# A log-sum-exp kernel: SyncE issues the first load ahead of the opening barrier

## The chip, the cores and the metric

One core of one Trainium2 chip. The metric is the device time of one execution in microseconds (us); the median of several executions is given, with its range. All executions of this study were in the fast state, with a granted clock of 1.00. A ratio is the mean time of one kernel's fast runs over the mean of the other kernel's fast runs in the same rounds, so it is not quite the ratio of the medians quoted beside it.

## The reference

```python
# x: float32 [32, 512, 1024]
max_x = np.max(x, axis=-1, keepdims=True)
return (max_x.squeeze(-1) + np.log(np.sum(np.exp(x - max_x), axis=-1))).astype(np.float32)
```

There are 16384 rows of 1024 numbers, 67.1 MB to read and 64 KB to write. Each of the 128 partitions holds 128 rows, `NC` in the code.

## The kernel before

The kernel reads the input once, through a ring of 48 rows per partition in SBUF. SyncE issues all loads; ScalarE takes the exponential in place; VectorE adds up most rows, and ScalarE itself some of them. The sums are taken without subtracting the maximum. A check at the end looks for sums that are out of range, and a slow path, not taken here, would repair them.

```python
    RING = 48
    loads = [
        "R8 R8", "R8 R8", "R8 R8", "R7 R6 A A", "R6 R5 A A A", "R5 R4 A", "R5 R4", "R5 T3",
        "R3 A A A", "R3 A", "R2 T2", "R3", "R1 A", "T2", "T1", "A", "A",
    ]                       # one string is one load; R: exp, then VectorE adds; A: ScalarE adds
# ... cut: the other tiles
    ring = big.tile([P, RING, d], fp32, name="ring")
    nc.scalar.preload_act_table_set("natural_log_exp_and_others")
    nc.vector.memset(ones, 1.0)
    nc.vector.memset(far, 100 * HIGH)

    def load(p0, c0, size):
        return nc.sync.dma_start(out=ring[:, p0 : p0 + size, :], in_=x_rows[:, c0 : c0 + size, :])
# ... cut
    for ops in loads:
        size = sum(s for _, s in ops)
        if p + size > RING:
            p = 0
        dma = load(p, c, size).ins
        for how, s in ops:
            v = ring[:, p : p + s, :]
            # ... cut: exp in place; reduce_sum of v on VectorE, or the accumulator of ScalarE
            c += s
            p += s
        tc.add_to_no_dep_group("loads", dma)
# ... cut
    nc.scalar.activation(out=res[:, EARLY:NC], in_=sumexp[:, EARLY:NC], func=AF.Ln)
    nc.sync.dma_start(out=out_view, in_=res)
# ... cut: the check of the sums, and the slow path
```

The opening of the program is not in this source. It begins with a barrier of all five engines: each engine executes a drain that reports to GpSimd, GpSimd sets four constants in memory, waits for the four reports, and releases all. Only then do the engines branch to the block that holds the code above. In the source above, the first three loads fill the ring (16 + 16 + 16 rows) and wait for no data and no slot; from the fourth on, a load waits until a slot is free.

## Time and profile before

| | before |
|---|---|
| time, median of the 3 runs known ahead of the prediction | 165.37 us (165.01 to 165.41) |
| span of the profiled execution (its own time: 164.92 us) | 163.1 us |
| first load issued / first data packet / sixteenth engine's first packet | 0.73 / 1.73 / 3.23 us |
| one 64 KB packet on one of the 16 DMA engines, steady | 2.42 us |
| last load has landed / tail after it | 159.01 / 4.1 us |

The span starts with the first instruction that the profile shows, which is SyncE's drain. The packets' times and the landing are from the trace's records of single DMA packets and of semaphore increments. A packet is a 64 KB piece, one partition's 16 rows in a large load. The records don't name the engine; the first 16 packets are taken to be on 16 engines, because all of them start before any of them ends.

From the page of the kernel before: the span; the busy share of the DMA engines in 40 slices of 4.08 us, in tenths; the rate in each slice; and the share that each engine has in the chain that ended last.

```profile
span 163.1 us, 198 instructions
...
DMA  6979989998998999899999999999999999999970
GB/s 257 514 321 450 514 370 402 514 418 354 514 418 354 514 438 407 377 482 482 450 394 422 436 420 402 402 450 434 434 418 442 422 440 400 426 423 421 409 314 18
...
DMA 64%; DVE 22%; ACT 12%; issue 1%; SPq 0%; PE 0%; DVEq 0%
```

The DMA engines are busy in every slice but the last, which is the tail after the loads. The first slice, with 257 GB/s, is short because the stream has not begun until 1.73 us, and the last two because it ends in them. The others scatter (321 to 514 GB/s) because whole packets are counted where they start. The chain names VectorE for 22%, because it follows loads back to the reductions that freed their slots; it doesn't say that the stream had run empty there.

From the table of waits of SyncE (what it waited for: us in total, how often, the longest) and of ScalarE:

```profile
SPq L72 <- DVE sumexp L99: 88.3, 7, 24.3
SPq L72 <- DMA ring<-in_x_dram: 41.1, 4, 20.9
...
SPq L197 <- PEq L197: 0.7, 1, 0.7
```

```profile
ACT ring L92 <- DMA ring<-in_x_dram: 42.9, 9, 21.0
```

SyncE waits 88 us for free slots, but all of this happens while earlier loads are in flight. The last line of SyncE's is the one at issue here: 0.7 us at the opening barrier, before any load. ScalarE waits 42.9 us for data.

From the instructions of the barrier, all under one source line (engine, operation, count; duration in ns, lowest/median/highest; first and last start in us; a "q" marks the engine's sequencer):

```profile
L197 POOLq EVENT_SEMAPHORE  x2: 17/17/17, 0.5 to 0.6; - x2
L197 SPq DRAIN  x1: 7/7/7, 0.0 to 0.0; - x1
...
L197 POOLq DRAIN  x1: 181/181/181, 0.3 to 0.3; - x1
...
L197 SPq EVENT_SEMAPHORE  x1: 17/17/17, 0.7 to 0.7; - x1
```

SyncE is at its drain at 0.0 us and passes the barrier at 0.65 us (0.7 as printed). GpSimd's own drain, which ends behind its four constants at 0.49 us, is what the others wait for.

From the timeline (start, duration, engine, line, operation):

```profile
0.24 0.10 POOL L197 MEMSET const-float32-0.0<- 128x1 f32 x1 [0.24 <-issue]
...
0.73 1.28 ACT L67 ACT_TABLE_LOAD   x1 [0.73 <-PEq L197]
0.73 1.33 SPq L72 DMA_DIRECT2D ring<-in_x_dram  x3
...
22.97 7.03 ACT L92 ACTIVATE ring<-ring 128x8192 f32<-128x8192 f32 x1 [20.95 <-DMA ring<-in_x_dram]
```

```profile
155.23 2.86 ACT L92 ACTIVATE ring<-ring 128x2048 f32<-128x2048 f32 x2 [0.22 <-DMA ring<-in_x_dram]
...
159.03 1.02 ACT L90 ACTIVATE last_exp<-ring 128x1024 f32<-128x1024 f32 x1
```

SyncE issues the first load at 0.73 us. ScalarE is ready at 2.01 us, after its table load, and has its first data at 22.97. At the end, it starts the last exponential at 159.03 us, 0.02 us after the last load has landed: the end too follows the data.

From the table of stretches, the one from 1 to 2 us (its last two numbers are the DMA share and the GB/s, again with whole packets counted where they start):

```profile
1.00:2.00 1.00, 0.00 (x0) 0.00 (x0) 0.00 (x0) 1.00 (x1) 0.00 (x0) 1.00 0.78 262
```

262 GB/s in 1 us are four packets of 64 KB: by 2 us, four of the 16 engines have begun.

### The profile page before, as it was taken

The page shows a single profiled execution, that of the slowest core. Times are in us where ns is not written, and L with a number is a line of the kernel's source. Part 1 is how long each engine was busy: PE and PEld are TensorE (multiplying, and loading weights), DVE is VectorE, ACT ScalarE, POOL GpSimd, SP SyncE. Part 2 cuts the span into 40 slices and gives each one's busy share as a digit, 9 for nine tenths or more (in the row PEclk, how much of TensorE's full clock was granted, in tenths as well). Part 3 has the DMA queues.
Part 4 walks back from the last instruction along what each step waited for, and adds up shares of the span by engine and source line. Part 5 has one row for each costly group of instructions (what it writes and reads, how often), then busy time and mean ns, then how long its engine had stood idle before and what let it go on. Part 6 is the DMA issues. An engine that isn't in the chain of part 4 may idle for free.

```text
span 163.1 us, 198 instructions
## 1 busy us (share of the span) xinstructions
PE 0.4 (0%) x6; PEld 0.2 (0%) x6; DVE 122.0 (75%) x44; ACT 116.8 (72%) x53; POOL 0.2 (0%) x4
## 2 busy tenths in 40 slices
PE   0000000000000000000000000000000000000001
PEld 0000000000000000000000000000000000000000
DVE  0000000699958999499999995999998999979893
ACT  3000039990699708995499829999969599999993
POOL 0000000000000000000000000000000000000000
DMA  6979989998998999899999999999999999999970
GB/s 257 514 321 450 514 370 402 514 418 354 514 418 354 514 438 407 377 482 482 450 394 422 436 420 402 402 450 434 434 418 442 422 440 400 426 423 421 409 314 18
DMA packets 2593, 67.18 MB, mean 412 GB/s; under 512 B 288, under 2 KB 416, under 8 KB 800
## 3 DMA queue, kind: packets, MB, share of 16 engines
q1 hardware_dynamic: 2592, 67.18, 95.9%
q14 instruction: 1, 0.01, 0.0%
HBM read 67.11 MB, written 0.07 MB: 412 GB/s over the span
## 4 chain that ended last, share of the span: by engine, by line
DMA 64%; DVE 22%; ACT 12%; issue 1%; SPq 0%; PE 0%; DVEq 0%
DMA ring<-in_x_dram 64%; DVE sumexp L99 20%; ACT ring L92 12%; DVE ring L104 1%; SPq L72 0%; DVE clamped L127 0%; PE count L140 0%; DVE bad L137 0%; DVE clamped L131 0%; DVE fine L143 0%; DVE bad L136 0%; PE count L141 0%; DVEq L127 0%
## 5 line engine op out<-in xcount | busy, mean ns | idle before, releaser
L99 DVE TENSOR_REDUCE sumexp<-ring 128x8 f32<-128x8192 f32 (+7 forms) x20 | 116.2, 5854 | 37.5 <-ACT ring L92 37.5
L92 ACT ACTIVATE ring<-ring 128x8192 f32<-128x8192 f32 (+7 forms) x24 | 101.7, 4283 | 42.9 <-DMA ring<-in_x_dram 42.9
L90 ACT ACTIVATE ring<-ring 128x1024 f32<-128x1024 f32 x12 | 12.5, 1040 | 0.0
L104 DVE SCALAR_TENSOR_TENSOR ring<-ring 128x512 f32<-128x512 f32 x8 | 5.1, 686 | 0.0
L90 ACT ACTIVATION_READ_ACCUMULATOR ring<-ring 128x1 f32 x12 | 2.2, 186 | 0.0
L67 ACT ACT_TABLE_LOAD x1 | 1.3, 1283 | 0.7 <-PEq L197 0.7
L90 ACT ACTIVATE last_exp<-ring 128x1024 f32<-128x1024 f32 x1 | 1.0, 1024 | 0.0
L104 DVE DVE_READ_ACCUMULATOR ring<-ring 128x1 f32 x8 | 0.7, 83 | 0.0
L68 DVE MEMSET ones<- 128x1 f32 x1 | 0.1, 59 | 0.8 <-PEq L197 0.8
L135 PE MATMUL count<-far,bad 128*1 128x1 f32 x2 | 0.2, 164 | 160.1 <-DVE clamped L131 160.1
L143 DVE TENSOR_SCALAR fine<-count 1x1 int32<-1x1 f32 x1 | 0.1, 145 | 0.3 <-PE count L141 0.3
L131 DVE SCALAR_TENSOR_TENSOR clamped<-clamped,sumexp 128x127 f32<-128x127 f32 x1 | 0.3, 292 | 0.0
L127 DVE TENSOR_SCALAR clamped<-sumexp 128x127 f32<-128x127 f32 x1 | 0.2, 228 | 0.1
L135 PEld LDWEIGHTS count<-far,bad 128*1 128x1 f32 x2 | 0.1, 80 | 160.1 <-DVE clamped L131 160.1
L119 ACT ACTIVATE res<-sumexp 128x104 f32<-128x104 f32 x1 | 0.3, 273 | 0.0
L121 ACT ACTIVATE res<-sumexp 128x24 f32<-128x24 f32 x1 | 0.2, 223 | 0.0
L136 DVE TENSOR_REDUCE bad<-ring 128x1 f32<-128x64 f32 x1 | 0.2, 215 | 0.0
L140 PE MATMUL count<-far,bad 128*1 128x1 f32 x2 | 0.2, 164 | 0.1
L141 PE MATMUL count<-ones,sumexp 128*1 128x1 f32 x2 | 0.2, 163 | 0.0
L90 ACT ACTIVATION_READ_ACCUMULATOR last_exp<-ring 128x1 f32 x1 | 0.2, 186 | 0.0
L137 DVE TENSOR_SCALAR bad<-bad 128x1 f32<-128x1 f32 x1 | 0.2, 153 | 0.0
L141 PEld LDWEIGHTS count<-ones,sumexp 128*1 128x1 f32 x2 | 0.1, 82 | 0.0
(7 smaller groups left out, 0.6 us busy)
## 6 DMA issues: line engine op xcount, KB each, us to landing
ring<-in_x_dram SPq DMA_DIRECT2D x1, 7680.0 KB, 32.4
ring<-in_x_dram SPq DMA_DIRECT2D x1, 7168.0 KB, 30.0
ring<-in_x_dram SPq DMA_DIRECT2D x1, 5120.0 KB, 31.4
ring<-in_x_dram SPq DMA_DIRECT2D x1, 4608.0 KB, 33.7
ring<-in_x_dram SPq DMA_DIRECT2D x1, 4096.0 KB, 29.3
ring<-in_x_dram SPq DMA_DIRECT2D x2, 2048.0 KB, 32.7
ring<-in_x_dram SPq DMA_DIRECT2D x1, 3072.0 KB, 36.3
ring<-in_x_dram SPq DMA_DIRECT2D x2, 1024.0 KB, 38.8
```

What stands on the lines that cost most here:

```text
L67: nc.scalar.preload_act_table_set("natural_log_exp_and_others")
L90: exp = nc.scalar.activation(out=o, in_=v, func=AF.Exp, accum_out=sums)
L92: exp = nc.scalar.activation(out=v, in_=v, func=AF.Exp)
L99: added = [nc.vector.reduce_sum(out=sums, in_=v, axis=AX.X)]
L104: nc.vector.scalar_tensor_tensor(out=lo, in0=lo, scalar=1.0, in1=ring[:, p + r, H:d], op0=ALU.mult, op1=ALU.add, accum_out=sums[:, r : r + 1],
L119: nc.scalar.activation(out=res[:, 0:EARLY], in_=sumexp[:, 0:EARLY], func=AF.Ln)
L121: nc.scalar.activation(out=res[:, EARLY:NC], in_=sumexp[:, EARLY:NC], func=AF.Ln)
L127: nc.vector.tensor_scalar(out=clamped[:, 0:LAST], in0=sumexp[:, 0:LAST], scalar1=LOW, scalar2=HIGH, op0=ALU.max, op1=ALU.min,)
L131: nc.vector.scalar_tensor_tensor(out=clamped[:, 0:LAST], in0=clamped[:, 0:LAST], scalar=0.0, in1=sumexp[:, 0:LAST], op0=ALU.bypass, op1=AL ...
L135: nc.tensor.matmul(count, lhsT=bad[:, 0:1], rhs=far, start=True, stop=False)
L136: nc.vector.reduce_max(out=bad[:, 2:3], in_=last_row[:, 0, 0 : d // 16], axis=AX.X)
L141: nc.tensor.matmul(count, lhsT=sumexp[:, LAST:NC], rhs=ones, start=False, stop=True)
```

## The change

The intent is to begin the load stream before the barrier is through. The first load reads the input and writes a part of the ring that nobody else has touched, so it doesn't need the barrier. The diff takes it out of its block and puts it ahead of SyncE's drain, when the program is finished:

```diff
         dma = load(p, c, size).ins
+        if c == 0:
+            first_load = dma
         for how, s in ops:
@@
+    def start_early(program):
+
+        blocks = program.main_func.blocks
+        here = next(b for b in blocks if any(i.name == first_load.name for i in b.instructions))
+        k = next(k for k, i in enumerate(here.instructions) if i.name == first_load.name)
+        assert not here.instructions[k].has_wait()
+        first = here.instructions.pop(k)
+        top = blocks[0].instructions
+        k = next(k for k, i in enumerate(top) if i.engine == mybir.EngineType.SP and "Drain" in type(i).__name__)
+        top.insert(k, first)
+
+    nc.at_finalize(start_early)
```

The order of instructions on the other four engines is the same in both programs; on SyncE one load stands ahead of the barrier instead of behind it.

## The prediction

> **What bounds the kernel now.** The load stream, from start to end. The first three loads wait only for the opening barrier. In the timeline SyncE issues the first at 0.73 us of the span (its drain, the first instruction of all, is at 0.00; the table of waits gives it 0.7 us for the barrier, released at 0.65). In the trace's packet records the first data packet starts at 1.73 us, the sixteenth engine's first one at 3.23; later each 64 KB packet takes 2.42 us, so 16 x 65536 B / 2.42 us = 433 GB/s. The Trainium skill, "DMA: Bandwidth & Descriptors", Specifications, gives 435 GB/s as the fabric's ceiling; the trace agrees. The windows show a DMA share of 0.88 to 1.06 in every ten microseconds from 10 to 150 us: no gap. Loads are issued 22 to 60 us before they land, so the queue always has work; the reductions that the chain of waits shows ahead of some loads (DVE 22%) free slots early enough. The last load lands at 159.01 us, the last exponential starts at 159.03, and a fixed tail of 4.1 us follows (exponential, logarithm, store, checks, closing barrier).
>
> **What the change does.** No work is removed or added. One load instruction moves from behind the barrier and the branch to ahead of SyncE's drain; it takes 0.38 us of the sequencer.
> - The first load is issued at about 0.00 instead of 0.73 us: 0.73 us won.
> - SyncE reaches the barrier at about 0.4 us. GpSimd, which gathers, ends its drain only at 0.49, so the barrier is delayed by 0 to 0.1 us. That doesn't matter: ScalarE, after its table load (1.28 us), waits until 22.97 us for data, and loads two and three aren't needed for some 20 us.
> - ScalarE and VectorE wait only on data or each other. Their starts, the freeing of slots and the later loads should shift together, so the 0.73 us should survive to the end.
>
> **On the critical path:** all of 0.73 us, give or take 0.2: 0.44% of 165.37 us. The three runs before spread over 0.4 us.
>
> **Predicted time:** 164.65 us, 8 times in 10 between 164.15 and 165.10. Chances: faster by over 2%: 1%; within 2%: 98%; slower by over 2%: 1%.
>
> **What in the profile would show it.**
> 1. SyncE's first load at 0.0 to 0.1 us, the first packet at about 1.0 us instead of 1.73.
> 2. The barrier releases at 0.65 to 0.75 us; loads two and three are issued right after, by 1.6 us.
> 3. The first exponential starts near 22.2 us instead of 22.97; the last load lands near 158.3; the tail stays 4.1 us; the span is about 162.4.
> 4. Packets still take 2.42 us.
>
> **What would make it wrong.**
> - SyncE's drain could wait for the load it follows. [...] Until the data has landed: the rings run empty between loads one and two, and the time rises by about 2 us (estimate: issue to first packet, 1.0, plus the spread of the engines' starts, 1.5, minus 0.73).
> - The clock of the measured time may start later than SyncE's first instruction; part of the gain would then not be seen.
> - The engines' staggered starts (1.5 us) may be set by something that doesn't move with the issue; the gain is then nearer 0.

## The result, and the profile after

| | before | after |
|---|---|---|
| time, median of 6 runs | 165.12 us (164.97 to 165.41) | 164.38 us (164.28 to 165.05) |
| ratio, with its 95% interval | | 0.9962 (0.9942 to 0.9981) |
| first load issued | 0.73 us | 0.00 us |
| first packet / sixteenth engine's first packet | 1.73 / 3.23 us | 1.01 / 2.27 us |
| steady 64 KB packet | 2.42 us | 2.42 us |
| first load has landed / last load has landed | 22.95 / 159.01 us | 22.04 / 158.82 us |
| time of the profiled execution itself / its span | 164.92 / 163.1 us | 164.75 / 163.0 us |

The changed kernel is faster by 0.74 us of the medians. The interval of the ratio is clear of 1.

The lines that answer to those of before. The page:

```profile
span 163.0 us, 198 instructions
...
DMA  8997998899899899989999979999999999999970
GB/s 306 467 515 338 434 515 386 386 515 418 354 515 418 354 499 483 392 362 452 450 450 450 450 322 483 382 417 407 434 434 458 402 428 420 430 417 421 412 294 20
...
DMA 64%; DVE 22%; ACT 12%; issue 0%; PE 0%; DVEq 0%
```

The first slice went from 257 to 306 GB/s. That is 49 GB/s over 4.08 us, or 0.20 MB, which at the steady rate would be 0.46 us; since whole packets are counted at their start, this view is too coarse for the question. The stretch from 1 to 2 us is finer:

```profile
1.00:2.00 1.00, 0.00 (x0) 0.00 (x0) 0.00 (x0) 1.00 (x1) 0.00 (x0) 1.00 2.80 983
```

983 GB/s are fifteen packets that start in it, where four did before. The packet records are finer still (below).

The waits of SyncE and of ScalarE, the barrier's instructions, and the timeline:

```profile
SPq L72 <- DVE sumexp L101: 88.5, 7, 24.3
SPq L72 <- DMA ring<-in_x_dram: 40.7, 4, 20.1
...
SPq L212 <- PEq L212: 0.2, 1, 0.2
```

```profile
ACT ring L94 <- DMA ring<-in_x_dram: 42.7, 9, 20.0
```

```profile
L212 POOLq EVENT_SEMAPHORE  x2: 17/17/17, 0.6 to 0.7; - x2
...
L212 POOLq DRAIN  x1: 181/181/181, 0.3 to 0.3; - x1
...
L212 SPq DRAIN  x1: 131/131/131, 0.4 to 0.4; - x1
L212 SPq EVENT_SEMAPHORE  x1: 17/17/17, 0.7 to 0.7; - x1
```

```profile
0.00 1.96 SPq L72 DMA_DIRECT2D ring<-in_x_dram  x3
0.23 0.10 POOL L212 MEMSET const-float32-0.0<- 128x1 f32 x1 [0.23 <-issue]
...
0.78 1.28 ACT L67 ACT_TABLE_LOAD   x1 [0.78 <-PEq L212]
...
22.07 7.03 ACT L94 ACTIVATE ring<-ring 128x8192 f32<-128x8192 f32 x1 [20.00 <-DMA ring<-in_x_dram]
```

```profile
155.06 2.85 ACT L94 ACTIVATE ring<-ring 128x2048 f32<-128x2048 f32 x2 [0.22 <-DMA ring<-in_x_dram]
...
158.87 1.01 ACT L92 ACTIVATE last_exp<-ring 128x1024 f32<-128x1024 f32 x1
```

SyncE's wait at the barrier fell from 0.7 to 0.2 us, because it now does its issue in that time. Its drain, which took 7 ns, takes 131 ns behind the load, and SyncE reaches the barrier after GpSimd's drain; the barrier releases SyncE at 0.70 instead of 0.65 us, and loads two and three are issued at 0.78 and 1.16 us. ScalarE's wait for data fell by only 0.2 us in this profile, and its last exponential starts only 0.17 us earlier. So the lead of 0.90 us that the first exponential had was mostly gone by the end of this one execution. It was one of the slower runs (164.75 us, the median is 164.38): its span is 163.0 us, while the record gives 162.5 or 162.6 us for four of the six executions. The experiments take this up.

Two measures from the packet and landing records are used from here on.

- The stream's **lag** is 10 us minus the time that the bytes moved by then would take at 433.6 GB/s. It says how late the stream is once all engines run. Within a packet the bytes are taken as moving evenly.
- The **rest** is the time from the landing of the first 16 rows to the landing of the last load.

### The profile page after: what moved, and what is told of

Read it like the earlier page. It is cut to its first block, busy times and chain, and to the rows that moved or that the text cites. A ratio compares the mean times of both kernels' runs of the same rounds, so it can differ in the third digit from the quotient of the medians.

```text
span 163.0 us, 198 instructions
## 1 busy us (share of the span) xinstructions
PE 0.4 (0%) x6; PEld 0.2 (0%) x6; DVE 122.0 (75%) x44; ACT 116.7 (72%) x53; POOL 0.2 (0%) x4
## 4 chain that ended last, share of the span: by engine, by line
DMA 64%; DVE 22%; ACT 12%; issue 0%; PE 0%; DVEq 0%
DMA ring<-in_x_dram 64%; DVE sumexp L101 20%; ACT ring L94 12%; DVE ring L106 1%; DVE clamped L142 0%; PE count L155 0%; DVE bad L152 0%; DVE clamped L146 0%; DVE fine L158 0%; DVE bad L151 0%; PE count L156 0%; DVEq L142 0%
```

## The experiments

Eleven kernels ran, each on one chip with runs of the kernel before. All gave correct results. The source edits are against the kernel before or the changed kernel, as stated.

| run | what | time, us | ratio to before | 16 rows' first issue, us | lag, us | first 16 rows landed, us | rest, us |
|---|---|---|---|---|---|---|---|
| before | | 165.12 | | 0.73 | 2.84 | 22.95 | 136.06 |
| after | | 164.38 | 0.9962 | 0.00 | 1.98 | 22.04 | 136.78 |
| e1_again | after, unedited | 164.54 | 0.9964 | 0.00 | 2.07 | 22.31 | 136.23 |
| e2_three_early | three loads early | 164.56 | 0.9962 | 0.00 | 2.11 | 22.32 | 136.41 |
| e3_late | all loads later | 168.56 | 1.0209 | 4.14 | 6.24 | 26.42 | 136.07 |
| e4_two_rows_early | 2 of 16 rows early | 164.10 | 0.9934 | 0.00 (2 rows), 0.78 | 1.78 | 21.81 | 136.38 |
| e5_scalar_late | after, ScalarE held | 164.54 | 0.9958 | 0.00 | 2.13 | 22.44 | 136.38 |
| e6_small_ahead | an unused 64 KB early | 165.48 | 1.0018 | 0.79 | 3.31 | 23.35 | 136.10 |
| e7_two_rows_split | 2 + 14 rows, none early | 164.98 | 0.9981 | 0.73 (2 rows), 1.16 | 2.47 | 22.45 | 136.80 |
| e8_one_row_early | 1 of 16 rows early | 165.07 | 0.9994 | 0.00 (1 row), 0.79 | 2.11 | 22.81 | 136.08 |
| e9_next_loads_held | after, loads 2 and 3 held | 164.43 | 0.9950 | 0.00 | 2.18 | 22.41 | 136.05 |
| e10_four_rows_early | 4 of 16 rows early | 164.12 | 0.9931 | 0.00 (4 rows), 0.79 | 1.84 | 21.80 | 136.42 |
| e11_two_rows_again | e4 once more | 164.20 | 0.9937 | 0.00 (2 rows), 0.78 | 1.85 | 21.73 | 136.36 |

Issues, lags, landings and rests are each of one profiled execution; times are medians of 5 or 6 runs. The medians of before were 165.12 us beside the result, 165.07 beside e1 to e4, 165.08 beside e5 to e8 and 165.20 beside e9 to e11.

My theory: the load stream bounds the kernel, and the end moves by what the start of the stream moves ("shift"). The rivals: what counts is when the other engines start, or ScalarE's first exponential; what counts is that an early issue wakes the DMA engines; or the difference is noise.

### The changed kernel again, and three loads early

e1_again is the changed kernel, unedited. e2_three_early puts all three loads that wait for nothing ahead of the drain:

```diff
-        if c == 0:
-            first_load = dma
+        if c < 48:
+            early_loads.append(dma)
@@ in start_early: the same move, for each of the three in order
+        for load_ins in early_loads:
```

> The changed kernel once more, unedited. Shift theory (the load stream bounds the kernel, and whatever its first issue moves, the end moves): ratio 0.9956 (0.73 of 165.1 us), and in a profile that catches a typical run a span 0.6 to 0.8 us shorter than before. Rival, noise: ratio within 0.999 to 1.001. It also shows whether the profiled run of the result (0.17 us shorter only, last landing 158.82) was an unlucky one.

> All three loads that wait for nothing are issued ahead of the barrier. SyncE then reaches the barrier about 0.85 us later (two more issues of some 0.43 us), so the barrier releases near 1.4 to 1.6 us and ScalarE and VectorE start that much later. Shift theory: the first issue is where it is in the changed kernel, so the time is the same as the changed kernel's within 0.15 us (ratio about 0.9956). Rival, the barrier counts (the gain depends on when the other engines start): 0.8 us slower than the changed kernel, ratio about 1.000. Second rival, each load's issue counts: a further 0.3 us or more faster.

e1_again repeated the gain: 164.54 us against 165.07, ratio 0.9964 (0.9949 to 0.9978). Noise as the rival is out. Its profile, of a run of 164.47 us, has its last landing at 158.54 us, 0.47 us before that of before, and a span of 162.7 us; I had expected a span shorter by 0.6 to 0.8 us, and it was shorter by 0.45.

e2_three_early was as fast, 164.56 us, ratio 0.9962 (0.9950 to 0.9975). From its timeline:

```profile
0.00 1.32 SPq L72 DMA_DIRECT2D ring<-in_x_dram  x3
...
1.73 1.28 ACT L67 ACT_TABLE_LOAD   x1 [1.73 <-PEq L214]
...
22.34 7.03 ACT L95 ACTIVATE ring<-ring 128x8192 f32<-128x8192 f32 x1 [19.33 <-DMA ring<-in_x_dram]
```

ScalarE's table load starts at 1.73 instead of 0.78 us, so the barrier was a good 0.9 us later, and no loss shows (the interval of the ratio reaches 0.2 us to either side). Both rivals had forecast more than that: 0.8 us lost if the times at which the other engines begin counted, a further 0.3 us won if the issues of loads two and three did.

### The first issue later

e3_late is the kernel before with one line more. The memset touches the slots of all three first loads, so SyncE has to wait for it.

```diff
     nc.vector.memset(far, 100 * HIGH)
+    nc.vector.memset(ring[:, 0:RING:16, :], 0.0)
```

> The kernel before, with the first three loads made to wait for a VectorE memset of 3072 elements per partition in their slots, after the barrier. The memset's duration sets the delay D of the first issue; I expect D between 0.8 and 3.5 us, to be read from its trace. Shift theory: the time grows by D, within 0.15 us. Rival, slack at the start (an early part of the delay is absorbed by the 7 us or so in which VectorE idles after its first start): less than half of D.

```profile
1.50 2.62 DVE L70 MEMSET ring<- 128x3072 f32 x1 [0.61 <-issue]
4.14 1.32 SPq L73 DMA_DIRECT2D ring<-in_x_dram  x3
26.50 7.03 ACT L93 ACTIVATE ring<-ring 128x8192 f32<-128x8192 f32 x1 [24.49 <-DMA ring<-in_x_dram]
```

The first issue is at 4.14 us, which is 3.41 us later than before. The ratio is 1.0209 (1.0195 to 1.0222). The median grew by 3.49 us (168.56 against 165.07), the lag by 3.40, and the last landing by 3.48 (162.49 against 159.01). A delay at the start of the stream is paid in full, and none is absorbed, although VectorE and ScalarE have idle time later.

### ScalarE held back

e5_scalar_late is the changed kernel with ScalarE kept busy until 24.2 us:

```diff
     nc.vector.memset(ones, 1.0)
+    for _ in range(21):
+        nc.scalar.activation(out=last_exp[:, 0, :], in_=ones[:, 0:1].to_broadcast([P, d]), func=AF.Exp)
```

> The changed kernel, with 21 exponentials of 1024 elements put on ScalarE ahead of the first real one (1.04 us each, so ScalarE is free at about 23.9 us; the first exponential starts there, 1.8 us after the 22.07 of the changed kernel). The loads start as in the changed kernel. Stream theory: ScalarE and VectorE have slack at the start, the first slots are still freed in time, and the time is the changed kernel's within 0.2 us (ratio 0.995 to 0.998). Rival, the chain of compute bounds (what the change gained is ScalarE's and VectorE's earlier start): 1.8 us slower than the changed kernel, ratio about 1.007.

```profile
0.00 48.88 SPq L74 DMA_DIRECT2D ring<-in_x_dram  x4
...
2.08 22.19 ACT L70 ACTIVATE last_exp<-ones 128x1024 f32<-128x1024 f32 x21
24.20 13.93 ACT L96 ACTIVATE ring<-ring 128x8192 f32<-128x8192 f32 x2
31.25 17.28 DVE L103 TENSOR_REDUCE sumexp<-ring 128x8 f32<-128x8192 f32 x2 [30.31 <-ACT ring L96]
```

The first real exponential starts at 24.20 instead of 22.07 us, and VectorE's first reduction at 31.25 instead of 29.13. The fourth load, which waits for that first slot, is issued at 48.56 us (46.43 in the changed kernel), still long before the third has landed at 61.29 us, so the queue doesn't run empty. The time is 164.54 us, ratio 0.9958 (0.9945 to 0.9971), as for the changed kernel. So 2.1 us on ScalarE and VectorE at the start cost nothing, while 3.4 us on the first issue cost 3.5. This is the pair of runs that shows that the stream bounds, and not the chain of compute.

### Which part of the first load has to be early

e4_two_rows_early cuts the first load in 2 and 14 rows and moves only the 2 rows. e8_one_row_early and e10_four_rows_early do the same with 1 and 4 rows. e7_two_rows_split has the cut alone and moves nothing (it lacks the last line of the diff of the change).

```diff
-        dma = load(p, c, size).ins
         if c == 0:
-            first_load = dma
+            first_load = load(p, c, 2).ins
+            dma = load(p + 2, c + 2, size - 2).ins
+        else:
+            dma = load(p, c, size).ins
@@ after add_to_no_dep_group("loads", dma), so that the first exponentials wait for both loads
+        if c == 16:
+            tc.add_to_no_dep_group("loads", first_load)
```

> Only 2 of the first load's 16 rows (1 MB, 8 KB a piece, about 2.4 us of the 16 engines at 433 GB/s) are issued ahead of the barrier; the other 14 rows and the next two loads follow after it, as one load more. Shift theory in its form for the stream: the small load covers the 0.78 us until the next issue, so the engines stay busy and the gain is that of the changed kernel, 0.5 to 0.75 us (ratio 0.9955 to 0.997), less what one more load and 8 KB pieces cost. Rival, it is the issue and the landing of the whole first load that count (ScalarE's first start, not the engines' first byte): its 14 rows are issued at 0.78 us, so no gain or a small loss, ratio 0.999 to 1.002.

> The split of the first load in 2 and 14 rows alone, all behind the barrier. The stream's lag (10 us minus the bytes that the packet records show by then over 433.6 GB/s) is 2.84 us in the kernel before, 1.98 and 2.07 in two profiles of the changed kernel, 1.78 with two rows early. If the split's and the early issue's parts add up, the lag is here about 2.5 us, and the time 0.3 us below before (ratio 0.998); two rows early is then the sum of the two. Rival, the split only pays when early: ratio 1.000 or above.

> As two rows early, but with one row (512 KB, 4 KB a piece, 1.2 us of the stream) ahead of the barrier and 15 behind it. The next load is issued at 0.78 us, so its first packet can start at about 1.8 us, before the small one is through (1.0 + 1.2 + the slow first piece, about 2.9 us): no gap. Expected is the time of two rows early within 0.2 us (ratio 0.993 to 0.995). If it is slower than two rows early by over 0.2 us, the small load is too small to bridge the gap.

> As two rows early, with four rows (2 MB, 16 KB a piece) ahead of the barrier and 12 behind it. One row early was uneven (164.14 to 165.98 us), two rows 163.92 to 164.23. If what matters is that the small load lasts until the pieces of the next one are in all 16 rings, four rows are as good and as steady as two (ratio 0.992 to 0.995, spread under 0.4 us); if small pieces at the start are what helps, four rows lie between two rows and the changed kernel (ratio 0.9945 to 0.9965).

> Two rows early once more, unedited, on another visit to a chip: ratio 0.9934 again, between 0.992 and 0.995, and clear of the changed kernel's 0.996.

e4 was faster than the changed kernel, which I had not expected: 164.10 us, ratio 0.9934 (0.9921 to 0.9947), where the changed kernel had 0.9964 (0.9949 to 0.9978) on the same chip beside the same runs of before. e11, the same kernel again, gave 0.9937 (0.9923 to 0.9951), and four rows early gave 0.9931 (0.9917 to 0.9945). So the large part of the first load may stay behind the barrier; the engines only have to get bytes early and keep getting them.

The two gains add up, about as expected. Cutting alone (e7) has ratio 0.9981 (0.9968 to 0.9994), the move alone 0.9962 and 0.9964; together they would give about 0.9944, and 0.9934, 0.9937 and 0.9931 were measured. In the lag it is 0.37 us for the cut, 0.66 to 0.86 for the move (in five profiles with the whole first load early and uncut), and 0.99 to 1.06 for both. The cut alone with four rows was not run.

The packet records show what the cut does at the start. The range is over the 16 engines. A packet that starts as another ends is taken as the next one of the same engine; in e7 some second packets start before the last engine's first.

| | first packets start, us | the slowest first packet takes, us | usual packet of that size, us |
|---|---|---|---|
| before (64 KB pieces) | 1.73 to 3.23 | 3.27 | 2.42 |
| after (64 KB) | 1.01 to 2.27 | 3.20 | 2.42 |
| e7, two rows, none early (8 KB) | 1.75 to 2.26 | 0.90 | 0.31 |
| e4, two rows early (8 KB) | 1.01 to 1.50 | 0.96 | 0.31 |

With 64 KB pieces the first and the last engine start 1.3 to 1.5 us apart in this table (0.9 to 1.5 over all profiles with such pieces, 0.9 in e2), with 8 KB pieces 0.5 to 0.6 us. In these four profiles the slowest first piece takes 0.6 to 0.9 us more than usual with either size; in the kernel before, the four engines that start last, at 3.14 to 3.23 us, have no slow one (2.42 to 2.45 us). Why large pieces start the engines further apart no run shows.

e8, one row early, missed its expectation: 165.07 us, but from 164.14 to 165.98 us over six runs, by far the widest range of all. Its profile, of a run of 164.85 us, shows a likely reason. The small load's last 4 KB piece is through at 2.99 us at the latest, but three of the large pieces start only at 3.30 to 3.66 us, and at 3.0 and 3.5 us only 13 and 14 packets are in flight instead of 16. The engines then stay apart to the end: the sixteen increments of the last load are spread over 1.46 us, against 0.77 in the kernel before and 0.56 in e4. By the expectation, one row is too small a load to bridge the gap. In e4 and e10 the large pieces follow the small ones with no gap. That this gap makes e8 uneven is argued from one profile; the fastest and the slowest of its runs were not profiled.

### Waking the DMA engines

e6_small_ahead is the kernel before with a load of 64 KB, into a tile that is overwritten later, ahead of the barrier. The three large loads stay behind it.

```diff
+    first_load = nc.sync.dma_start(out=res, in_=x_rows[:, 0, 0:NC]).ins
     c = 0
     p = 0
@@ start_early as in the change
```

> The kernel before, with a load of 64 KB that nobody needs (0.15 us of the stream) ahead of the barrier; the three large loads are issued after the barrier at about 0.78 us. Shift theory: no gain, 0 to 0.2 us slower than before. Rival, the early issue only wakes the 16 engines (their first packets are the slow ones, 3.0 to 3.3 us against 2.42, and they start 1.3 to 1.5 us apart): the small load takes that cost, the large load's first packets take 2.42 us and start close together, and the time falls by 0.3 us or more although the load of 8 MB is issued no earlier.

165.48 us, ratio 1.0018 (1.0005 to 1.0031): slower by about 0.3 us as mean ratio, a little more than the 0 to 0.2 us expected. The first 64 KB pieces start at 2.03 to 3.35 us and the slowest takes 3.83. So an earlier transfer did not make the first large pieces fast, nor bring the engines together. An early issue alone is worth nothing; the bytes have to be useful ones.

### Loads two and three held

e9_next_loads_held is the changed kernel, with loads two and three made to wait for a VectorE memset in their slots. It asks whether their issues cause the slow and scattered first packets.

```diff
     nc.vector.memset(far, 100 * HIGH)
+    nc.vector.memset(ring[:, 16:RING:8, :], 0.0)
```

> The changed kernel, with loads two and three made to wait for a VectorE memset (4096 elements per partition, estimate 3.5 us from the 2.62 us that 3072 took), so they are issued near 5 us instead of 0.78 and 1.16. The first load has the engines to itself until then; its 8 MB last until about 21 us, so nothing runs empty. Question: do the issues of loads two and three cause the slow first packets (2.7 to 3.2 us instead of 2.42) and the staggered starts (1.0 to 2.3 us) of the changed kernel? If they do: nearly all first packets take 2.42 us, the lag of the stream falls from 2.0 or 2.1 to about 1.5 us, and the time is 0.3 to 0.5 us below the changed kernel's (ratio 0.993 to 0.995). If they don't: ratio 0.9955 to 0.9970 as the changed kernel, lag 2.0 to 2.1.

Loads two and three were issued at 5.26 and 5.64 us. The first packets started at 1.01 to 2.15 us and took up to 3.31 us, and the lag was 2.18 us, much as in the changed kernel (1.98 and 2.07; I had written 2.0 to 2.1). So those issues are not the cause. The ratio was 0.9950 (0.9937 to 0.9963), a little lower than I had written for this outcome, and the five runs lay within 0.1 us (164.39 to 164.49).

### What is lost later

The rests in the large table fall in two groups. Five profiles (before, e3, e6, e8, e9) have 136.05 to 136.10 us. The other eight have 136.23 to 136.80. The 64 KB pieces that began after 6 us and took over 30 ns more than the usual 2.42 us tell the groups apart: the five have 0, 5, 1, 0 and 0 of them, in this order; the eight have from 9 (e10) to 87 (e7). The 64 KB pieces are only a sample, since after some 80 us the loads are smaller. Taken over pieces of all sizes, the time above the usual for their size, per engine and from 6 us on, exceeds that of the profile before by 0.49 us in the result's profile, 0.21 in e1_again, 0.38 in e2, 0.52 in e7 and 0.00 in e9; the rests exceed it by 0.72, 0.17, 0.35, 0.74 and -0.01. From 6 to 154 us, 16 packets were in flight for over 99% of the time in these profiles and in that of before (never fewer than 14). So slow packets cost most of the time, and not gaps in the stream; the excess is a mean over the engines, while a landing waits for the slowest. In the result's profile 7 of its 15 came between 50.0 and 50.7 us; in e1_again 8 of its 14 between 40.4 and 41.3. The lead of the result's profile over the one before shrinks, and over half of the loss comes after the fourth load, where 55 smaller pieces between 79 and 120 us were slow (3 before):

| landing, us | first load | second | third | fourth | last |
|---|---|---|---|---|---|
| before | 22.95 | 42.27 | 61.62 | 79.77 | 159.01 |
| after | 22.04 | 41.35 | 60.83 | 79.19 | 158.82 |
| e1_again | 22.31 | 41.65 | 61.15 | 79.33 | 158.54 |

These losses are not tied to the early issue: e7, which moves nothing early, has the largest, and e8 and e9, which do, have none. What slows these packets stays open. Losses of 0.2 to 0.7 us also explain why one profile of each kernel is a poor measure of a gain of this size.

## Why the prediction was right

- **Issue and start of the stream.** Predicted: first load at 0.0 to 0.1 us, first packet at about 1.0. Measured: 0.00 and 1.01.
- **The barrier.** Predicted: released between 0.65 and 0.75 us, 0 to 0.1 us later, at no cost. Measured: 0.70. e2_three_early delayed it by 0.9 us more, and no cost showed.
- **All of 0.73 us on the critical path.** e3_late shows a slope of one for a delay (3.41 us in, 3.49 out), and e5_scalar_late shows that compute has slack at the start. The medians fell by 0.74 us beside the result and by 0.53 in e1_again; as mean ratios both are about 0.6 us. The 0.73 us, give or take 0.2, held; the intervals of the two ratios, 0.3 to 1.0 and 0.4 to 0.8 us, are wider than that. The time itself came out 0.27 us below the 164.65 predicted, mostly because the three runs known before had a median of 165.37 us and all six 165.12.
- **The start-up of the 16 engines.** I feared that their staggered starts would not move. They moved with the issue, and closed up a little (1.50 us apart before, 1.26 and 1.06 in the two profiles after, 0.87 to 1.30 in e2, e5 and e9). The lag fell by 0.86 and 0.77 us, and by 0.73, 0.71 and 0.66 in those three: over the five, by what the issue moved.
- **The last landing near 158.3 us and a span of 162.4.** This was missed in the two profiles: 158.82 and 158.54, spans of 163.0 and 162.7; four of the result's six executions had spans of 162.5 or 162.6, so typical ones came close. The part of the argument that "the 0.73 us should survive to the end" left out that an execution can lose 0.2 to 0.7 us to slow packets on the way. The tail stayed at 4.1 us.
- **The drain.** It did wait for something, 131 ns instead of 7, but not for the data. The bad case didn't come.

## What to carry to other kernels

When a kernel is bound by its load stream from the first byte to the last, every microsecond before the first issue is paid in full, as e3 showed here, so a load that depends on nothing belongs ahead of whatever the program waits for at its start. Only a small part of it has to be early, by the argument from e8 enough to last until the next load's pieces can start on all engines: here 1 MB and 2 MB were enough, and 0.5 MB was not. Before crediting such a gain to a step, delay that step on purpose and delay its rival as well; a slope of one against a slope of zero says more than one pair of profiles, which here scattered by as much as the gain.

The kernel with two or four rows early beats both kernels: 164.10 to 164.20 us, against 164.38 and 164.54 for the change in its two settings and 165.07 to 165.20 for before.

## What the Trainium skill lacked or had wrong

- "DMA: Bandwidth & Descriptors", Specifications, gives about 0.6 us as the first-byte latency of a load from SyncE, without saying from when. From the start of the issuing instruction to the first packet it was 1.00 us here (0.73 to 1.73 before, 0.00 to 1.01 after); less the instruction's own 0.38 us it is 0.63, which agrees. That is the first engine of 16; the last one began 0.9 to 1.5 us later with 64 KB pieces, and 0.5 to 0.6 with 8 KB pieces. No page has this spread.
- No page has it that an engine's first packet can be slower: up to 3.4 us where 2.42 is usual (3.8 in e6, behind a small load), up to 0.96 where 0.31 is.
- The same page, Specifications, has two ceilings, 435 GB/s for the fabric and about 358 GB/s of HBM for one core. With one core running, the steady packets gave 433 GB/s, so only the first held here; the page "HBM Reference" says so too, with about 425 GB/s for a core that streams alone.
- "VectorE: DVE Perf Modes", The DRAIN you can't avoid, gives some 12 ns, constant, for the drains of the runtime's preamble and postamble. The drains of the program's own opening barrier took 7 to 10 ns, but SyncE's 131 ns behind a load, and GpSimd's 181 ns behind its memsets. The page doesn't speak of these.
- "Runtime: NRT & Kernel Launch", The ~15µs preamble/postamble breakdown, lists barriers of the runtime around the kernel. The program's own opening barrier, 0.65 us from SyncE's drain to its release, is on no page, nor is it said that a load may stand ahead of it.
